# A two-layer decoder step on one core: 8 KB weight pieces, a longer weight ring, one sum for the samples' attention, and an earlier sort of the experts

## Chip, core and metric

One NeuronCore of a Trainium2 chip runs the whole step as one program. The metric is the device time of one execution in microseconds (us), the median of several runs. TensorE (PE) does the matrix products, VectorE (DVE) and ScalarE (ACT) the elementwise work, GpSimd (POOL) a part of that and the indirect DMAs, SyncE (SP) issues most of the other DMAs. Weights and tables come from HBM through 16 DMA engines that all queues share.

## What is computed

The step runs a prompt of 512 tokens and 8 samples of one token each through two layers with shared weights; the width is 1024. All data are fp32.

```python
# layer 0 mixer: convolution and differential attention; the samples read a paged cache of 1024 positions
gb, gc, xin, q, k, v = jnp.split(x @ w_in, EVEN_SPLITS, axis=-1)
a = jax.nn.softmax(s, axis=-1).reshape(b, H_B, 2, tq, tk)
a = a[:, :, 0] - lam * a[:, :, 1]
o = jnp.einsum('bhqk,bkhe->bqhe', a, v)            # H_B = 4 heads of 128 values
y = jnp.concatenate([y_conv, rms_norm(o, subln_w) ...], axis=-1) @ w_out
# layer 1 mixer: mLSTM in chunks
# tail of both layers
x = layer_norm(ALPHA * x + mix)
x = layer_norm(ALPHA * x + hier_moe(x))
x = x + sigmoid(x @ wpg) * (p @ wpp)

def hier_moe(x, ...):      # 4 groups of 4 experts: best group, two best experts in it
    for e in range(16):
        hid = silu(xt @ w_gate[e]) * (xt @ w_up[e])      # 1024 -> 512
        y = y + gate[:, e:e + 1] * (hid @ w_down[e])     # 512 -> 1024
```

## The kernel before

A layer is a mixer (layer 0's projections and attention to about 222 us, its output projection, "mix 0", to about 321 us), the experts (layer 0 to about 626 us; layer 1 from about 981 to 1288 us), and the tail with the gated projection of `p`.

**Experts.** They are done in 16 slots `e`. Slots 0 and 1 hold experts 0 and 1; slots 2 to 15 hold the others, sorted by the number of their tokens on the chip (`cnt`, `key`, `lt`, `sr`, `sel`, `eid`, lines 1143 to 1149), and the sorted numbers become integers in `eii` (line 1150). SP reads a number from `eii` into a register (line 1388) before it can issue that slot's loads. Odd slots from 3 on (`SMALL`) take up to 64 tokens and multiply in fp32 (lines 1253, 1297). The nine others, the dense slots, take up to 128 tokens and use three products of a high and a low part (`mm3`, lines 142 to 144); ACT and DVE make the two parts of each weight (lines 137 and 138). `prepare(e)` makes a slot's one-hot matrix `oh` (line 1088), its row indices `ix` (1099) and gathers its tokens from `xd` by an indirect DMA on POOL (1103). `tokens` transposes the gathered rows on PE (`tr_block`, line 266; the gathered rows are the stationary operand), `hidden` makes silu times up (its ACT step is line 1263 in dense slots), `hidden_T` transposes that, and `down` multiplies by the last weight and scatters the sum. Slot `e`'s down product stands behind slot `e+1`'s up product, except that slot 13's stands before slot 14's up product.

**Weight buffers.** A slot reads 6 MB: gate, up and down of 2 MB, each in two loads of 1 MB (`load_w`, line 155, issued by SP, some by POOL). A load goes to the next buffer of a ring (`wbuf`, `wpools`, `wturn`) and waits until whoever read the buffer's last content is done. The ring has 13 buffers of 1 MB: 3 of `wp2`, 4 of `wp3`, two halves of `wps[1]` ("b"), two of "xl" and two of "xh". Eight loads (gate and up of slots 0 and 1) are issued in the mixer. At slot `ESW = 10` the ring becomes `RS = "2b"`, which takes `wp2` (3 buffers) and the two halves of `wps[1]` in turn. In a load, partition `p` gets row `k*128+p` for each `k` ("(k p)"), so one contiguous piece is a row: 2 KB for gate and up, 4 KB for down.

**Samples' attention in mix 0.** The weights of all 8 samples stand in `a4`. `v_step` takes one sample `b`: eight products (line 669) of `a4` with the sample's cached values, in a PSUM tile of its own; a mask (line 673) that keeps this sample's rows and, per head, its columns; a product with a one-hot matrix (line 677) that sums over partitions; and an addition to `acco`. The values come by indirect DMAs on POOL, 2 MB a sample. `mix_tile` is a generator that makes the output projection for one of five row groups `m`; steps of the samples' attention run between its steps.

Of the kernel before, what the change touches and what calls it, by code (L numbers as in the profile page):

```python
# [14 lines left out]
OP = mybir.AluOpType  # L15
# [36 lines left out]
ESW = 10  # L52
G0 = 2
RS = "2b"
# [66 lines left out]
class K:  # L121
# [233 lines left out]
    def even(self):  # L355
# [5 lines left out]
        with tc.tile_pool(name="mz", bufs=1) as mz, tc.tile_pool(name="mx", bufs=1) as mx, tc.tile_pool(name="mx2", bufs=2) as mx2:  # L361
# [299 lines left out]
            def v_step():  # L661
                if not vq:
                    return
                b, wv = vq.pop(0)
                pv = self.tp()
                for hf in range(2):
                    w = wv[hf].rearrange("p (t c) -> p t c", t=4)
                    for t in range(4):
                        TE.matmul(pv[32 * t:32 * t + 32, :], self.a4[:, 4 * hf + t, :], w[:, t, :],
                                  start=(hf == 0), stop=(hf == 1))  # L670
                mk = mx2.tile([128, 512], F32, name="mk", bufs=1)
                h4 = lambda a: a.rearrange("p (h c) -> p h c", h=4)
                V.scalar_tensor_tensor(h4(mk), h4(pv), self.c("bmask")[:, b:b + 1],
                                       self.c("maskhp")[:, :, None].to_broadcast([128, 4, 128]), op0=OP.mult, op1=OP.mult)
                yield
                po = self.tp()
                TE.matmul(po[:NS, :], self.onf_b(mx, b), mk, start=True, stop=True)
                if b == 0:
                    V.tensor_copy(acco, po[:NS, :])
                else:  # L680
                    V.tensor_add(acco, acco, po[:NS, :])
# [40 lines left out]
            def decode_tail():  # L722

                while vq:
                    yield from v_step()
                    v_load()
                    yield
                os_ = mx2.tile([NS, 4, 128], F32, name="os", tag="aT")
                for h in range(4):
                    V.scalar_tensor_tensor(os_[:, h, :], vt[:NS, 4, h * 128:(h + 1) * 128], self.an[:, h:h + 1],  # L730
                                           acco[:, h * 128:(h + 1) * 128], op0=OP.mult, op1=OP.add)
                yield from norm_o(os_, NS, 4, 0, slice(TP, T))
                self.moe_load(0, 1 + NW2, 1 + NW2 + NW3)
# [24 lines left out]
    def onf_b(self, p, b):  # L758
        if b == 0:
            self.eb = p.tile([128, NS, NS], F32, name="eb")  # L760
            self.V.tensor_copy(self.eb, self.c("mask8").rearrange("p (a b) -> p a b", a=8))
        return self.eb[:, b, :]

# [16 lines left out]
    def moe_load(self, i, a, b):  # L780

        rows = lambda w: [w[h * 512:h * 512 + 512, :].rearrange("(k p) c -> p k c", p=128) for h in range(2)]
        ws = [v for e in range(2) for n in ("w_exp_gate", "w_exp_up") for v in rows(self.A[n][i, e])]
        self.early += [self.load_w(v) for v in ws[a:b]]
# [68 lines left out]
    def mix_all(self, i, y, tags, before, after_first, own=None):  # L853
# [3 lines left out]
        parts = self.mix_split(own)  # L857
        for _ in range(MS):
            next(parts)
# [15 lines left out]
    def mix_tile(self, i, m, y, tags, tile, before):  # L875
# [41 lines left out]
        acc = [self.acc() for _ in range(2)]  # L917
# [37 lines left out]
        if m == 0:  # L955
            for k in range(8):
                if k == 6:
                    while before():
                        self.advance()
                    load()  # L960
                for hf in range(2):
                    product(k, hf)
                yield
            add(0)
            add(1)
        else:
# [92 lines left out]
    def moe(self, i):  # L1059
# [5 lines left out]
        with tc.tile_pool(name="exp", bufs=2) as p2:  # L1065
# [58 lines left out]

            prepare(0)
            prepare(1)

            order = ExitStack()
            order.enter_context(tc.issue_after(self.ix_last.ins))
            order.enter_context(tc.issue_after(self.gather_last.ins))  # L1130
# [19 lines left out]
            V.tensor_copy(eii, eid[:, 2:])  # L1150
# [7 lines left out]

            rs = p2.tile([128, 5, ns], F32, name="rs", bufs=1)
# [54 lines left out]
            def tokens(xg, small=False):  # L1214

                if small:
                    xT = p2.tile([128, 4, 2, HCAP], F32, name="xT", tag="gh")
                    ps = self.tp().rearrange("p (a b) -> p a b", a=4)
                    for j in range(4):
                        self.tr_block(ps[:, j, :], xg[:, j * 128:(j + 1) * 128], 128)  # L1220
# [4 lines left out]
                for g in range(2):  # L1225
                    ps = self.tp().rearrange("p (a b) -> p a b", a=4)
                    for j in range(4):
                        self.tr_block(ps[:, j, :], xg[:, (g * 4 + j) * 128:(g * 4 + j + 1) * 128], 128)
# [38 lines left out]
            def hidden_T(hid, small=False):  # L1267
                if small:
                    hx = p2.tile([128, 4, HCAP], F32, name="hx", tag="hh", bufs=1)
                    ps = self.tp()[:, 0:4 * HCAP].rearrange("p (a b) -> p a b", a=4)  # L1270
                    for j in range(4):
                        self.tr_block(ps[:, j, :], hid[:, j * 128:(j + 1) * 128], HCAP)
# [5 lines left out]
                for j in range(4):  # L1278
                    self.tr_block(ps[:, j, :], hid[:, j * 128:(j + 1) * 128], 128)
# [3 lines left out]
            def down(ix, gate, hx, src, now, small, end=False):  # L1283

                pd = self.acc()
                ws = [self.load_w(v, now) for v in src] if end else None
# [30 lines left out]
            def dyn(ev, n, r):  # L1317

                return [A[n][i][bass.ds(ev, 1), h * r:h * r + r, :].rearrange("o (k p) c -> p (o k) c", p=128) for h in range(2)]
# [57 lines left out]
            rows = lambda w, n: [w[h * n:h * n + n, :].rearrange("(k p) c -> p k c", p=128) for h in range(2)]  # L1377
# [3 lines left out]
            for e in range(NE):  # L1381
# [8 lines left out]
                if e == ESW:  # L1390

                    self.wpools, self.wturn = self.ring(RS), 0
# [29 lines left out]
                if last and e != NE - 2:  # L1422
                    down(*last[:2], hx, *last[3])
# [627 lines left out]
```

## Time and profile before

| | before |
|---|---|
| median of 3 runs | 1384.08 us (1380.81 to 1386.75) |
| profiled execution | 1380.0 us, span 1378.2 us |
| PE busy | 1263.3 us, 92% of the span |
| DVE, ACT, POOL busy | 863.5, 628.7, 254.0 us |
| moved by DMA | 338.73 MB, mean 246 GB/s |

The span is the time from the first to the last event on the core. The busy share of an engine is a mean over the stages; what holds a stage is seen in its own windows and waits. The DMA share of a window is the mean busy share of the 16 DMA engines.

### The profile page before, as it was taken

Reading aid. Unit: us, or ns where it says so; the run is one execution under the profiler, and the core shown is the slowest. Engines: PE = TensorE matmul, PEld = TensorE weight load, DVE = VectorE, ACT = ScalarE, POOL = GpSimd, SP = SyncE. Lnnn points to the kernel's source line nnn. Section 1 sums busy time; section 2 is a strip of 40 time slices with the busy share of each in tenths; the row PEclk is TensorE's granted clock in tenths of the full one; section 3 lists DMA queues with packets and bytes.
Section 4 is the critical chain, followed back from the end, with each engine's and each line's share of the span. In section 5 each row is a group of like instructions: output and inputs, shape, how many; then the busy total and the mean of one; then the engine's idle time right before and its main releaser. Section 6 shows DMA issues by size and latency. Waiting matters only on the chain. (4 is left out here: it accounts for less than half of the span.)

```text
span 1378.2 us, 20912 instructions
## 1 busy us (share of the span) xinstructions
PE 1263.3 (92%) x7884; PEld 967.4 (70%) x7884; DVE 863.5 (63%) x1515; ACT 628.7 (46%) x1053; POOL 254.0 (18%) x242
## 2 busy tenths in 40 slices
PE   7989999995899999988999999999589999998897
PEld 7988876563766655547979999878367665555686
DVE  4689985557976654435645456874698565443572
ACT  3224664223665544436553333323366554443562
POOL 1033312314122221001230000112312112100113
PEclk9999999997999999999999999999789999999899
DMA  8568645873999989998332224493399999999911
GB/s 284 159 199 293 221 176 210 311 275 136 355 349 370 367 298 363 372 364 249 109 112 82 74 65 127 158 338 124 137 328 332 377 361 315 343 369 355 286 49 40
DMA packets 157449, 338.73 MB, mean 246 GB/s; under 512 B 16095, under 2 KB 54459, under 8 KB 153246
## 3 DMA queue, kind: packets, MB, share of 16 engines
q1 hardware_dynamic: 138974, 271.28, 55.3%
q0 software_dynamic: 18224, 65.98, 15.3%
q8 instruction: 64, 1.05, 0.3%
q14 instruction: 43, 0.35, 0.1%
q10 hardware_dynamic: 144, 0.07, 0.0%
HBM read 313.66 MB, written 32.81 MB: 251 GB/s over the span
## 5 line engine op out<-in xcount | busy, mean ns | idle before, releaser
L138 DVE TENSOR_TENSOR w<-w,sh 128x1024 fp32r<-128x1024 f32 x224 | 267.3, 1221 | 117.5 <-ACT sh L137 98.8
L137 ACT CAST sh<-w 128x1024 fp32r<-128x1024 f32 x224 | 227.9, 1048 | 175.8 <-PE acc L234 104.8
L143 PE MATMUL acc<-w,gh 128*128 128x512 f32 x288 | 119.2, 414 | 7.3 <-DVE w L138 7.3
L142 PE MATMUL acc<-sh,gh 128*128 128x512 f32 x288 | 118.6, 412 | 3.4 <-ACT sh L137 3.4
L144 PE MATMUL acc<-sh,gl 128*128 128x512 f32 x288 | 117.1, 407 | 0.0
L1253 PE MATMUL acc<-w,xT 128*64 128x512 f32 x432 | 109.7, 597 | 1.3 <-DMA w<-in_w_exp_up 1.3
L234 PE MATMUL acc<-xh,sh 128*128 128x256 f32 (+1 forms) x384 | 84.1, 296 | 5.8 <-ACT sh L137 2.6
L234 PE MATMUL acc<-x2h,w 128*128 128x256 f32 (+1 forms) x384 | 86.8, 288 | 1.6 <-DMA wgx<-in_w_ple_gate 0.8
L234 PE MATMUL acc<-xh,w 128*128 128x256 f32 (+1 forms) x384 | 80.3, 291 | 1.1 <-DVE w L138 1.1
L234 PE MATMUL acc<-x3h,sh 128*128 128x256 f32 (+1 forms) x384 | 81.1, 291 | 0.0
L234 PE MATMUL acc<-xl,sh 128*128 128x256 f32 (+1 forms) x384 | 80.6, 290 | 0.0
L234 PE MATMUL acc<-x3h,w 128*128 128x256 f32 (+1 forms) x384 | 78.5, 284 | 0.0
L234 PE MATMUL acc<-x3l,sh 128*128 128x256 f32 (+1 forms) x384 | 78.3, 284 | 0.0
L1253 PEld LDWEIGHTS acc<-w,xT 128*64 128x64 f32 x432 | 32.3, 136 | 59.6 <-issue 54.0
L1103 POOL DMA_INDIRECT w<-xd,ix x32 | 47.4, 1480 | 140.6 <-DVE gs L1113 84.1
L143 PEld LDWEIGHTS acc<-w,gh 128*128 128x128 f32 x288 | 56.3, 195 | 24.0 <-DVE w L138 11.3
L142 PEld LDWEIGHTS acc<-sh,gh 128*128 128x128 f32 x288 | 56.1, 195 | 18.6 <-ACT sh L137 5.2
L234 PEld LDWEIGHTS acc<-xh,sh 128*128 128x128 f32 x384 | 62.4, 195 | 7.6 <-ACT sh L137 2.9
L1314 POOL DMA_INDIRECT ya<-y,ix x18 | 29.3, 1627 | 205.7 <-ACT y L1313 205.7
L234 PEld LDWEIGHTS acc<-x2h,w 128*128 128x128 f32 x384 | 64.4, 188 | 2.5 <-issue 1.3
L144 PEld LDWEIGHTS acc<-sh,gl 128*128 128x128 f32 x288 | 56.4, 196 | 13.0
L234 PEld LDWEIGHTS acc<-xh,w 128*128 128x128 f32 x384 | 61.7, 194 | 1.4 <-DVE w L138 1.3
(540 smaller groups left out, 2932.5 us busy)
## 6 DMA issues: line engine op xcount, KB each, us to landing
w<-in_w_exp_gate SPq DMA_DIRECT2D x56, 1024.0 KB
w<-in_w_exp_up SPq DMA_DIRECT2D x50, 1024.0 KB
w<-in_w_exp_down SPq DMA_DIRECT2D x50, 1024.0 KB
wpair<-in_w_exp_up SPq DMA_DIRECT2D x14, 1024.0 KB
w<-in_w_in_even SPq DMA_DIRECT2D x12, 1024.0 KB
w<-in_w_in_odd SPq DMA_DIRECT2D x12, 1024.0 KB
wpair<-in_w_exp_down SPq DMA_DIRECT2D x10, 1024.0 KB
wpair<-in_w_exp_gate SPq DMA_DIRECT2D x8, 1024.0 KB
```

The source lines that it names most:

```text
L137: a = self.S.copy(h, src)
L138: self.sp_last = a, self.V.tensor_sub(l, src, h.bitcast(F32))
L142: self.T.matmul(ps, ah, bh, start=start, stop=False)
L143: self.T.matmul(ps, ah, bl, start=False, stop=False)
L144: self.mm3_last = self.T.matmul(ps, al, bh, start=False, stop=stop)
L234: self.mm_last = self.T.matmul(ps[t], a[:, k, :], b[:, k, t0[t]:t1[t]], start=(k == 0 and i == 0), stop=(k == nk - 1 and i == 2))
L1103: self.gather_last = G.indirect_dma_start(out=xg, out_offset=None, in_=rows2(xd) if small else xd, in_offset=bass.IndirectOffsetOnAxis(ap= ...
L1253: TE.matmul(ps[z * HCAP:(z + 1) * HCAP, :], xT[:, a, hf, :], ws[z][:, a, :], start=(hf == 0 and a == 0), stop=(hf == 1 and a == 3))
L1314: G.indirect_dma_start(out=ya, out_offset=bass.IndirectOffsetOnAxis(ap=ix[:, 0:1], axis=0), in_=y, in_offset=None, bounds_check=T - 1, oob ...
```

## The change

Five edits. (1) The ring of 13 buffers stays until slot 13, and then goes on in the same order without "b" and "xh" (9 buffers), where before it was exchanged for "2b" at slot 10. (2) In a load, partition `p` gets neighbouring rows ("(p k)"), so that its piece is 8 KB for gate, up and down; to match, the transposes take every fourth column of the gathered rows (16 bytes apart) and every second column of the hidden values (8 bytes apart). (3) The samples' weights are masked per sample (`ab`, 128x256 elements on DVE) before the products; all samples add into one PSUM tile, half of the accumulator `macc[0]`, and one `v_sum` masks heads and sums over partitions. `macc` is one pair of accumulators for all row groups, and group 0's residual addition comes before its last `yield`. (4) The sort by counts stands between `prepare(0)` and `prepare(1)`. (5) The four down loads of slots 0 and 1 (`wd`) are issued before `prepare(0)`, slot 0's on POOL and slot 1's on SP.

```diff
@@
-ESW = 10
+ESW = 13
 G0 = 2
-RS = "2b"
...
@@ v_step, v_sum
                 b, wv = vq.pop(0)
-                pv = self.tp()
+
+                if b == 0:
+                    self.ab = mx2.tile([128, 2, 8, NS, 4], F32, name="ab", tag="mk", bufs=1)
+                ab = self.ab[:, b % 2]
+                V.tensor_tensor(ab, self.a4.rearrange("p t (b h) -> p t b h", h=4),
+                                self.c("mask8").rearrange("p (a b) -> p a b", a=8)[:, b, None, :, None].to_broadcast([128, 8, NS, 4]), op=OP.mult)
+                ab = ab.rearrange("p t b h -> p t (b h)")
+                yield
+                pv = self.macc[0][:, 1, :]
                 for hf in range(2):
                     w = wv[hf].rearrange("p (t c) -> p t c", t=4)
                     for t in range(4):
-                        TE.matmul(pv[32 * t:32 * t + 32, :], self.a4[:, 4 * hf + t, :], w[:, t, :],
-                                  start=(hf == 0), stop=(hf == 1))
+                        TE.matmul(pv[32 * t:32 * t + 32, :], ab[:, 4 * hf + t, :], w[:, t, :],
+                                  start=(b == 0 and hf == 0), stop=(b == NS - 1 and hf == 1))
+
+            def v_sum():
                 mk = mx2.tile([128, 512], F32, name="mk", bufs=1)
                 h4 = lambda a: a.rearrange("p (h c) -> p h c", h=4)
-                V.scalar_tensor_tensor(h4(mk), h4(pv), self.c("bmask")[:, b:b + 1],
-                                       self.c("maskhp")[:, :, None].to_broadcast([128, 4, 128]), op0=OP.mult, op1=OP.mult)
+                V.tensor_tensor(h4(mk), h4(self.macc[0][:, 1, :]), self.c("maskhp")[:, :, None].to_broadcast([128, 4, 128]), op=OP.mult)
                 yield
                 po = self.tp()
-                TE.matmul(po[:NS, :], self.onf_b(mx, b), mk, start=True, stop=True)
-                if b == 0:
-                    V.tensor_copy(acco, po[:NS, :])
-                else:
-                    V.tensor_add(acco, acco, po[:NS, :])
+                TE.matmul(po[:NS, :], self.c("bmask"), mk, start=True, stop=True)
+                V.tensor_copy(acco, po[:NS, :])
@@ decode_tail
+                yield from v_sum()
...
@@ moe_load, moe (rows, dyn)
-        rows = lambda w: [w[h * 512:h * 512 + 512, :].rearrange("(k p) c -> p k c", p=128) for h in range(2)]
+        rows = lambda w: [w[h * 512:h * 512 + 512, :].rearrange("(p k) c -> p k c", p=128) for h in range(2)]
...
-                return [A[n][i][bass.ds(ev, 1), h * r:h * r + r, :].rearrange("o (k p) c -> p (o k) c", p=128) for h in range(2)]
+                return [A[n][i][bass.ds(ev, 1), h * r:h * r + r, :].rearrange("o (p k) c -> p (o k) c", p=128) for h in range(2)]
@@ moe
+            rows = lambda w, n: [w[h * n:h * n + n, :].rearrange("(p k) c -> p k c", p=128) for h in range(2)]
+            wd = [[self.load_w(v, z == 1) for v in rows(A["w_exp_down"][i, z], 256)] for z in range(2)]
             prepare(0)
-            prepare(1)
-
-            order = ExitStack()
-            order.enter_context(tc.issue_after(self.ix_last.ins))
-            order.enter_context(tc.issue_after(self.gather_last.ins))
+            first = ExitStack()
+            first.enter_context(tc.issue_after(self.ix_last.ins))
...
-            V.tensor_copy(eii, eid[:, 2:])
+            eii_last = V.tensor_copy(eii, eid[:, 2:])
...
+            first.enter_context(tc.issue_after(eii_last.ins))
+            prepare(1)
+            first.close()
+
+            order = ExitStack()
+            order.enter_context(tc.issue_after(self.ix_last.ins))
+            order.enter_context(tc.issue_after(self.gather_last.ins))
@@ tokens, hidden_T (the small and the dense form alike)
-                        self.tr_block(ps[:, j, :], xg[:, (g * 4 + j) * 128:(g * 4 + j + 1) * 128], 128)
+                        self.tr_block(ps[:, j, :], xg[:, g * 512 + j:(g + 1) * 512:4], 128)
...
-                    self.tr_block(ps[:, j, :], hid[:, j * 128:(j + 1) * 128], 128)
+                    self.tr_block(ps[:, j, :], hid[:, j // 2 * 256 + j % 2:(j // 2 + 1) * 256:2], 128)
@@ loop over slots
                 if e == ESW:
 
-                    self.wpools, self.wturn = self.ring(RS), 0
+                    k, ws = self.wturn % len(self.wpools), self.wpools
+                    self.wpools, self.wturn = [w for w in ws[k:] + ws[:k] if w not in (self.wps[1], "xh")], 0
...
-                    down(*last[:2], hx, *last[3])
+                    down(*last[:2], hx, *last[3], ws=wd[e - 1] if e < 3 else None)
```

PE's program in mix 0 has, before, products by `a` (the tile `a4`; `w` are the cached values) into a `tps` tile, and behind them the sum over partitions (L677); L142 to L144 are the output projection.

```order
L142 MATMUL acc<-xl,yh 128x512
L143 MATMUL acc<-w,yh 128x512
L144 MATMUL acc<-xl,yl 128x512
L677 MATMUL tps<-mk,eb 8x512
L266 MATMUL tps<-cst,xw_2651 128x128 x4
L142 MATMUL acc<-xh,yh 128x512
L143 MATMUL acc<-w,yh 128x512
L144 MATMUL acc<-xh,yl 128x512
L142 MATMUL acc<-xh,yh 128x512
L143 MATMUL acc<-w,yh 128x512
L144 MATMUL acc<-xh,yl 128x512
L669 MATMUL tps<-w,a_2548 32x512 x8
```

The program of the change has at that place products by the masked `ab` straight into the accumulator, and no sum behind them.

```order
L265 MATMUL tps<-cst,xw_2651 128x128 x4
L141 MATMUL acc<-xh,yh 128x512
L142 MATMUL acc<-w,yh 128x512
L143 MATMUL acc<-xh,yl 128x512
L141 MATMUL acc<-xh,yh 128x512
L142 MATMUL acc<-w,yh 128x512
L143 MATMUL acc<-xh,yl 128x512
L676 MATMUL acc<-w,ab 32x512 x8
```

The eight L677 products are gone from between the projection's products; one sum (L685) comes after the last sample, and the eight products by the values are as many as before, of the same shape.

SP's program where layer 0's experts begin, before: the last rows of the mixer's result (`xd`, `ya`), then the first expert number and slot 2's loads.

```order
L1006 DMA xd_90<-xw_3231 8x1024
L1008 DMA ya_92<-xw_3231 8x1024
L1388 TENSOR_LOAD eii
L1388 ISA x2
L155 ISA
L155 DMA wpair<-in_w_exp_gate 128x4x512
L155 ISA
L155 DMA wpair<-in_w_exp_gate 128x4x512
L155 ISA
L155 DMA wpair<-in_w_exp_up 128x4x512
```

The same place in the change, as far as the second of the register loads that now follow one another:

```order
L154 DMA wpair<-in_w_exp_down 128x2048 x2
L1009 DMA xd_90<-xw_3189 8x1024
L1011 DMA ya_92<-xw_3189 8x1024
L1397 TENSOR_LOAD eii
L1397 ISA x2
L154 ISA
L154 DMA wpair<-in_w_exp_gate 128x2048
L154 ISA
L154 DMA wpair<-in_w_exp_gate 128x2048
L1397 TENSOR_LOAD eii
L1397 ISA x2
L1397 TENSOR_LOAD eii
```

Slot 1's two down loads moved ahead of the stores of the last rows, and the other 13 reads of `eii`, which stood one before each later slot's loads, moved up: nine stand between slot 2's last gate load and its first up load, and four behind the next read of a number (`nbi`).

DVE's program at that place, before: behind the rank of the tokens (`rank`) come both slots' `oh` and `ix`, and the sort is mixed with other routing work, so that `eii` is written 23 rows behind `rank`.

```order
L1056 SCALAR_TENSOR_TENSOR rank<-tps,Mb 128x80
L1088 TENSOR_TENSOR oh<-slf,rank 128x640 x2
L1099 TENSOR_SCALAR ix<-tps 128x1 x2
L1165 TENSOR_REDUCE sgx<-L 128x5
L1143 COPY cnt<-tps 128x16
L1166 TENSOR_TENSOR sge<-L,sgx 128x20
L1165 TENSOR_REDUCE sex<-el 128x5
L1144 SCALAR_TENSOR_TENSOR key<-cnt,cst 128x16
```

In the change:

```order
L1059 SCALAR_TENSOR_TENSOR rank<-tps,Mb 128x80
L1091 TENSOR_TENSOR oh<-slf,rank 128x640
L1102 TENSOR_SCALAR ix<-tps 128x1
L1146 COPY cnt<-tps 128x16
L1147 SCALAR_TENSOR_TENSOR key<-cnt,cst 128x16
L1148 TENSOR_TENSOR lt<-key 128x196
L1149 TENSOR_REDUCE sr<-lt 128x14
L1150 TENSOR_TENSOR sel<-sr,cst 128x196
L1151 TENSOR_TENSOR lt<-sel,cst 128x196
L1152 TENSOR_REDUCE eid<-lt 128x14
L1153 CAST eii<-eid 128x14
L1091 TENSOR_TENSOR oh<-slf,rank 128x640
```

The sort now follows slot 0's indices at once, and slot 1's `oh` and `ix` come behind `eii`.

## Rows read from the trace of the kernel before

**Rows 1.** windows of 25 us in layer 0's experts (engines busy, clock, DMA share, GB/s).

```profile
450.00:475.00 25.00, 25.00 (x127) 13.97 (x127) 13.76 (x19) 10.83 (x15) 5.39 (x3) 1.00 1.03 367
...
575.00:600.00 25.00, 21.24 (x91) 14.50 (x92) 15.01 (x14) 14.26 (x17) 3.12 (x2) 0.93 1.05 377
```

**Rows 2.** timeline of ACT, layer 0: the hidden activations of slots 4 to 14.

```profile
423.73 0.60 ACT L1263 ACTIVATE hid<-acc 128x512 f32<-128x512 f32 x1 [1.77 <-PE acc L144]
...
455.76 0.60 ACT L1263 ACTIVATE hid<-acc 128x512 f32<-128x512 f32 x1 [4.97 <-PE acc L144]
...
487.74 0.60 ACT L1263 ACTIVATE hid<-acc 128x512 f32<-128x512 f32 x1 [4.91 <-PE acc L144]
...
522.50 0.60 ACT L1263 ACTIVATE hid<-acc 128x512 f32<-128x512 f32 x1 [4.58 <-PE acc L144]
...
559.76 0.60 ACT L1263 ACTIVATE hid<-acc 128x512 f32<-128x512 f32 x1 [4.49 <-PE acc L144]
...
602.66 0.60 ACT L1263 ACTIVATE hid<-acc 128x512 f32<-128x512 f32 x1 [4.72 <-PE acc L144]
```

**Rows 3.** the same in layer 1: slots 8 and 14.

```profile
1149.10 0.60 ACT L1263 ACTIVATE hid<-acc 128x512 f32<-128x512 f32 x1 [4.91 <-PE acc L144]
...
1264.72 0.60 ACT L1263 ACTIVATE hid<-acc 128x512 f32<-128x512 f32 x1 [5.34 <-PE acc L144]
```

**Rows 4.** waits of SP's queue, 345 to 615 us: line <- releaser: total us, times, longest.

```profile
SPq L155 <- DVE w L138: 84.6, 23, 8.1
SPq L155 <- PE acc L1253: 51.6, 13, 10.7
```

**Rows 5.** timeline of SP around slot 10: weight loads as they are issued.

```profile
478.99 6.16 SPq L155 DMA_DIRECT2D w<-in_w_exp_down  x2
...
498.14 0.99 SPq L155 DMA_DIRECT2D w<-in_w_exp_gate  x2
```

**Rows 6.** windows of 5 us (columns as in the first group).

```profile
275.00:280.00 5.00, 4.90 (x25) 2.15 (x23) 2.82 (x5) 0.59 (x1) 0.99 (x1) 1.00 1.01 408
...
490.00:495.00 5.00, 4.86 (x41) 2.44 (x41) 1.10 (x2) 2.09 (x4) 0.64 (x1) 1.00 0.65 255
...
505.00:510.00 5.00, 4.78 (x21) 3.56 (x21) 4.97 (x8) 3.75 (x4) 1.43 (x1) 1.00 1.05 395
```

**Rows 7.** timeline of PE: slot 13's down product.

```profile
589.09 3.65 PE L1297 MATMUL acc<-w,hx 128*64 128x512 f32 x16
```

**Rows 8.** mix 0: PE's groups and a timeline of PE.

```profile
L677 PE MATMUL tps<-mk,eb 128*8 128x512 f32 x16 | 8.2, 594 | 0.0
...
248.98 1.02 PE L677 MATMUL tps<-mk,eb 128*8 128x512 f32 x2
249.94 0.66 PE L266 MATMUL tps<-cst,xw 128*128 128x128 f32 x4
```

**Rows 9.** the 25-us window in mix 0's middle.

```profile
250.00:275.00 25.00, 25.00 (x144) 12.78 (x144) 12.61 (x19) 5.30 (x7) 9.96 (x9) 1.00 0.88 321
```

**Rows 10.** transposes on PE's timeline; loads of stationary operands in the experts and mix 0.

```profile
432.22 1.09 PE L266 MATMUL tps<-cst,w 128*128 128x128 f32 x8
433.15 0.39 PE L1093 MATMUL tps<-idr,oh 128*128 128x1 bf16 x10
...
L266 PEld LDWEIGHTS tps<-cst,w 128*128 128x128 f32 x84 | 9.6, 141 | 5.8 <-issue 4.9
...
L934 PEld LDWEIGHTS acc<-w,yh 128*8 128x8 f32 x14 | 1.3, 90 | 1.3
```

**Rows 11.** timelines of DVE, SP and PE at layer 0's first slots.

```profile
338.27 0.17 DVE L1150 CAST eii<-eid 128x14 int32<-128x14 f32 x1
...
327.15 0.29 SPq L1006 DMA_DIRECT2D xd<-xw  x1
...
336.93 2.79 PE L266 MATMUL tps<-cst,w 128*128 128x128 f32 x12 [4.64 <-DMA w<-xd,ix]
```

**Rows 12.** SP's register loads of an expert number, all 28.

```profile
L1388 SPq TENSOR_LOAD <-eii x28: 262/274/1084, 338.6 to 1249.8; - x28
```

More of the change, by code (lines that the diff above doesn't have):

```diff
@@ L756, in even @@
             self.mix_all(0, y, tags, lambda: self.pend, after_first)
[L758 to L762, printed above, removed]
     def mixer_pools(self):
@@ L857, in mix_all @@
         parts = self.mix_split(own)
+        self.macc = [self.acc() for _ in range(2)]
         for _ in range(MS):
@@ L916, in mix_tile @@
             y_split(1)
-        acc = [self.acc() for _ in range(2)]
+        acc = self.macc
         st = tile("lst", [128, 2, 6], F32)
@@ L962, in mix_tile @@
                     product(k, hf)
-                yield
+                if k < 7:
+                    yield
             add(0)
             add(1)
+            yield
         else:
@@ L1219, in tokens @@
                     for j in range(4):
-                        self.tr_block(ps[:, j, :], xg[:, j * 128:(j + 1) * 128], 128)
+                        self.tr_block(ps[:, j, :], xg[:, j::4], 128)
                     S.copy(xT.rearrange("p a z b -> p a (z b)"), ps)
@@ L1271, in hidden_T @@
                     for j in range(4):
-                        self.tr_block(ps[:, j, :], hid[:, j * 128:(j + 1) * 128], HCAP)
+                        self.tr_block(ps[:, j, :], hid[:, j // 2 * 256 + j % 2:(j // 2 + 1) * 256:2], HCAP)
                     self.hid_last = S.copy(hx, ps)
@@ L1278, in hidden_T, with down @@
                 for j in range(4):
-                    self.tr_block(ps[:, j, :], hid[:, j * 128:(j + 1) * 128], 128)
+                    self.tr_block(ps[:, j, :], hid[:, j // 2 * 256 + j % 2:(j // 2 + 1) * 256:2], 128)
                 self.hid_last = self.split(hh, hl, ps)
                 return hh, hl
-            def down(ix, gate, hx, src, now, small, end=False):
+            def down(ix, gate, hx, src, now, small, end=False, ws=None):
                 pd = self.acc()
-                ws = [self.load_w(v, now) for v in src] if end else None
+                ws = [self.load_w(v, now) for v in src] if end else ws
                 if end:
@@ L1375, in overflow @@
                         down(ix, gate, hidden_T(hidden(pgu)), dyn(ev, "w_exp_down", 256), True, False)
-            rows = lambda w, n: [w[h * n:h * n + n, :].rearrange("(k p) c -> p k c", p=128) for h in range(2)]
             last = None
```

## The prediction

> **What bounds the kernel now.** Busy shares first: PE is busy for 92% of the span, so time is won only by taking work from PE, or where PE waits or runs slower than it could. Next I looked for stretches of the second kind, in windows over the experts of layer 0. At 450 to 475 us PE is busy for 25.00 of 25 us at full granted clock (1.00). At 575 to 600 us it is busy for 21.24 at a mean clock of 0.93, while the DMA engines stand at 1.05 [rows 1]. So the experts are bound by PE at first and by their weights at the end.
>
> The size of that is read from the hidden activation of every second slot, since a dense and a small slot make a pair with equal work. From slot 4 to 6 it takes 32.03 us, from 6 to 8 31.98, then 34.76, 37.26 and 42.90 [rows 2]. 32.0 us is what a pair takes where PE never waits. Layer 1 behaves alike: from slot 8 to 14 it takes 115.62 us [rows 3], in layer 0 114.92.
>
> Why do the weights come late? SP's queue, which issues the loads, waits mostly for readers of old buffers: 84.6 us for DVE's splitting and 51.6 us for the small slots' products [rows 4]. At slot 10 the change of the ring is seen: after the down loads issued at 478.99 us nothing is issued until 498.14 us [rows 5], because the short ring first has to wait for buffers that are still to be read. In that hole the DMA share falls to 0.65 (255 GB/s), and then it is at 1.05 [rows 6], too late to make up for it. So at the end DMA bandwidth is the limit, but the loss began as a want of free buffers.
>
> **1 and 2. The ring and the pieces.** With 13 buffers until slot 13 the hole at 484 to 498 us is not there. Can the DMA then keep up? A pair needs 12 loads, 12.58 MB. With 2 KB pieces the engines moved 395 GB/s at a share of 1.05, that is 376 at 1.00 [rows 6], so 33.5 us a pair. To that come its gathers and scatters: 192 rows of 4 KB in and as many out, 1.6 MB, 4.2 us at that rate. 37.7 us against PE's 32.0: the store of loaded weights shrinks by 5.7 us a pair. The windows agree that it shrinks: 367 GB/s [rows 1] are 11.7 MB in 32 us, less than the weights alone. With the early down loads 12 MB are in the buffers at the start, 32 us of PE's work; over the 6 pairs from slot 2 to 14 that would be used up (34 us). Now the pieces: the gathers of cached values in mix 0 bring 8 KB pieces already, 408 GB/s at 1.01, 404 at 1.00 [rows 6]. A pair's weights then take 31.1 us, with the 4.2 us 35.3, and 6 pairs use 20 of the 32 us. So with both edits the weights stay ahead of PE to the end; the pieces have no term of their own, but without them the last pair would lose some us. From slot 13 on nine buffers are left, 24 us of PE's work, and the switch itself forces no wait, since the order goes on.
>
> Slot 14's pair is longer than 32.0 also when PE is the limit, since slot 13's down product stands ahead of its up product: 3.65 us [rows 7]. Three pairs then take 3 x 32.0 + 3.65 = 99.65 us, where before they took 114.92 and 115.62. That is **-15.3** in layer 0 and **-16.0** in layer 1. Bounds: nothing is won (new holes), or all of it.
>
> The price of the pieces is on PE. The transposes of gathered rows now read every fourth column as the stationary operand. There are 9 x 8 + 7 x 4 = 100 of them in a layer, 200 in all, and 64 in a layer of hidden values at every second column. Eight take 433.15 - 432.22 = 0.93 us, 0.116 us each, and loading such an operand takes 141 ns beside the products [rows 10]. No operand of PE in this kernel is read with a stride, so the price is bounded. Below: nothing, since the same columns go into the same array. Above: a load of 8 columns takes 90 ns, one of 128 takes 141 [rows 10], so the columns themselves cost (141 - 90) / 120 = 0.42 ns each, 54 ns for 128; if reading takes four times as long, as wide as the stride, that is 163 ns more for each, 33 us for 200. PE has no slack there [rows 1], so it would all be paid. I take **0**: nearer to the lower end, since most of the 141 ns does not depend on the columns, and the product of the transpose before runs meanwhile.
>
> [...]
>
> **3. Samples' attention.** PE loses 7 of the 8 sums over partitions. A sum takes two passes, from 248.98 to 249.94 us, 0.96 us in all, and the 16 rows are all there are [rows 8]: 7 x 0.96 = 6.7 us of PE's time. The eight products a sample stay. PE is full in the middle of mix 0 (25.00 of 25 us), so this comes off the end unless something else is just behind. The DMA is at 0.88 there with 321 GB/s [rows 9]: it can run 12% faster and no more, and each sample's 2 MB must come before the next step. In 99 us PE can win 6.7%, so the gathers come near their limit without reaching it. I take three quarters, **-5.0**; bounds 0 (the gathers are the limit) and -6.7. On DVE the eight masks of `ab` have 256 columns where the removed ones had 512, so DVE gets no more work (12.61 of 25 us busy [rows 9]).
>
> **4 and 5. Sort and early down loads.** At the start of layer 0's experts `eii` is written at 338.27 us while PE begins its transposes at 336.93 after a wait of 4.64 us for slot 0's gathered rows [rows 11]. PE thus does not wait for the sort. With the sort earlier, some 4 us of it, slot 2's loads come 4 us earlier, which feeds the store and not PE. Against it stand three delays. Slot 1's indices and gather come behind the sort, 2 to 4 us later, and its transposes stand early in PE's order, so PE can wait for them: 0 to 2 us. Nine register loads of an expert number (each 0.27 us, with what belongs to it about 0.45 [rows 12]) now stand between two loads, 4 us of SP, covered by slot 2's 2 MB of gate weights and slot 1's 2 MB in flight. The last stores to `xd` (327.15 us [rows 11]) are issued behind slot 1's two down loads on the same queue, and the gathers wait for these stores: 2 MB at 404 GB/s is 5 us if the queue serves strictly in order, nothing if the down loads have gone out before. I take **+1.0** for both layers together, with bounds -4 and +8.
>
> **The sum.** 1380.0 us is the profiled execution's own time. 1380.0 - 15.3 - 16.0 - 5.0 + 1.0 = 1344.7 us. The runs' median is 1384.1, 4.1 us above the profiled one, so I forecast **1349 us**, 2.5% less. A difference under 0.5% (7 us) is about what a measurement here cannot tell from none.
>
> **The rivals.**
>
> *A. The strided transposes are slow.* For it speaks that the load of the operand (141 ns) is longer than the spacing (116 ns), so little can be hidden behind the product; against it that only 54 ns of it are columns. Twice the reading is 200 x 0.054 = 11 us, 1356, on the median's basis **1360 us**; three times 22 us, **1371 us**; four times 33 us, **1382 us**.
>
> *B. The same, so slow that the kernel loses.* The gain of the other parts is 35.3 us, so this decides from 35.3 / 200 = 0.18 us more for each transpose, a spacing of 0.29 us. If the whole spacing of 0.116 us grows with the stride, four times, it is 0.35 x 200 = 70 us: 1415, on the median's basis **1419 us**. The other engines could hide nothing of it, as PE is the limit; for it speaks only that nothing here shows such a read.
>
> *C. The DMA stays the limit at the end.* If the pairs from slot 8 on go on taking 34.76 us, as the pair before the hole's effect shows in full [rows 2], three of them and slot 13's product take 107.9 us: 7.0 us are won in layer 0 and 7.7 in layer 1. With mix 0's 5 and the start's 1 it would be 1380.0 - 18.7 = 1361, on the median's basis **1365 us**. For it speaks a share that is at 1.03 already while PE is full [rows 1], and that the store is counted from estimates: at the old rate it is used up just at slot 14. Against it stand the 12 us that the pieces leave.
>
> *D. The ring does what it should, and mix 0 and the starts give it back.* The gathers limit mix 0 (nothing won) and the stores behind the down loads cost 4 us in each layer: 1380.0 - 31.3 + 8 = 1357, on the median's basis **1361 us**.
>
> **Chances and range.** The forecast's case (1336 to 1357) has 0.60, A 0.16, C 0.11, D 0.07, B 0.06. The lower end takes the whole of mix 0 (-1.7 more), the start's -4 (5 less than taken) and 6 us for stretches whose clock no longer drops: 1336. The upper end takes in A at three times the reading with 6 us on top: 1377. Outside are B and the upper part of A. Faster by over 0.5% are the forecast, C, D and A up to three times: 0.87. A at four times is within 0.5%: 0.07. B is slower: 0.06.
>
> **What would show it.** The ring: pairs of 32.0 us up to slot 12, about 35.7 to slot 14, no hole in SP's loads near slot 10, PE busy for all of 25 us at 575 us, DMA share under 1. The pieces: rates near 404 GB/s at a share of 1.00 in the experts. The strides: eight transposes at a spacing of 0.12 us (right), of 0.17 to 0.28 (A) or more (B); then pairs get longer everywhere, by 12 transposes' extra. Mix 0: shorter by 5 us, one L685 in place of eight sums, its DMA share near 0.95; a share at 1.0 with PE waiting for cached values is D. The starts: `eii` at about 334 us, first product no later than 339 us. The forecast is wrong if the transposes are slow, or if the nine buffers at the end leave a new hole.

## The result, and the profile after

The change is slower: 1397.94 us (median of 4 runs, 1397.11 to 1402.96) against 1382.44 us of before in the same rounds, a ratio of 1.011 (1.008 to 1.015). The forecast was 1349 us, 2.5% faster.

The profiled execution has a span of 1401.2 us, 23.0 more than before. In order of time: 3.4 us arise ahead of mix 0, where nothing was changed (PE's granted clock is 0.50 from 108.7 to 115.5 us, where before has 1.00). Mix 0 takes as long as before (-0.3). The first hidden activation of layer 0 comes 2.5 us later behind mix 0; from it to slot 15's, the experts take 258.2 us in place of 251.5. Near 710 us, in layer 1's mixer, 3.3 us are won back; layer 1 then starts its experts 6.9 us later and needs 258.8 us in place of 252.0 for them.

The timeline of ACT in the changed kernel, layer 0. The rows with `hid` on 128x512 answer to [rows 2]; the others show what stands around the hidden activation of two small slots, 5 (443.49) and 9 (511.90).

```profile
439.99 1.99 ACT L136 CAST sh<-w 128x1024 fp32r<-128x1024 f32 x2
443.49 0.59 ACT L1270 ACTIVATE hid<-acc 64x512 f32<-64x512 f32 x1 [1.50 <-PE acc L1263]
445.03 1.05 ACT L136 CAST sh<-w 128x1024 fp32r<-128x1024 f32 x1 [0.96 <-PE acc L143]
...
462.14 0.60 ACT L1273 ACTIVATE hid<-acc 128x512 f32<-128x512 f32 x1 [5.00 <-PE acc L143]
...
496.92 0.60 ACT L1273 ACTIVATE hid<-acc 128x512 f32<-128x512 f32 x1 [4.60 <-PE acc L143]
...
511.90 0.59 ACT L1270 ACTIVATE hid<-acc 64x512 f32<-64x512 f32 x1 [6.78 <-PE acc L1263]
512.39 1.98 ACT L136 CAST sh<-w 128x1024 fp32r<-128x1024 f32 x2
...
534.05 0.60 ACT L1273 ACTIVATE hid<-acc 128x512 f32<-128x512 f32 x1 [4.58 <-PE acc L143]
...
571.33 0.60 ACT L1273 ACTIVATE hid<-acc 128x512 f32<-128x512 f32 x1 [4.60 <-PE acc L143]
...
614.53 0.60 ACT L1273 ACTIVATE hid<-acc 128x512 f32<-128x512 f32 x1 [5.45 <-PE acc L143]
```

Pairs from slot 6 on take 34.78, 37.13, 37.28 and 43.20 us; before it was 31.98, 34.76, 37.26, 42.90 [rows 2]. The slow pairs thus begin one pair earlier, and the fast one before them (32.5, to 462.14) is half a microsecond longer. In slot 5 the splits of the waiting down weights are done when the hidden activation starts; in slot 9 ACT has been idle for 6.78 us and begins the splits only behind it; they stand behind it in the program, and no wait for a transfer is recorded ahead of them. PE's timeline shows what goes with this.

```profile
438.23 1.23 PE L265 MATMUL tps<-cst,w 128*128 128x128 f32 x8
439.30 0.39 PE L1096 MATMUL tps<-idr,oh 128*128 128x1 bf16 x10
...
442.81 0.60 PE L1263 MATMUL acc<-w,xT 128*64 128x512 f32 x2
443.34 0.50 PE L141 MATMUL acc<-sh,hh 128*128 128x512 f32 x1
...
445.39 0.69 PE L265 MATMUL tps<-cst,hid 64*128 64x64 f32 x4
...
507.41 4.45 PE L1263 MATMUL acc<-w,xT 128*64 128x512 f32 x18
513.27 0.69 PE L265 MATMUL tps<-cst,hid 64*128 64x64 f32 x4 [1.41 <-DVE hid L1271]
...
515.09 0.77 PE L142 MATMUL acc<-w,hh 128*128 128x512 f32 x1
515.66 0.63 PE L143 MATMUL acc<-sh,hl 128*128 128x512 f32 x1
```

At 443 us the waiting down product (L141) follows the up product (L1263) at once, and the transposes of slot 5's own hidden values (`hid`) come eight products later, when ACT and DVE have made them. At 512 us there are no split weights yet, and on PE the transposes of `hid` come next: PE stops for 1.41 us until DVE has made slot 9's hidden values, and then a product takes 0.63 us where it otherwise takes 0.40. So the late order is one of PE's program as well as of ACT's. Windows of the same kernel (columns as in [rows 1]):

```profile
375.00:400.00 25.00, 25.00 (x128) 20.61 (x127) 23.67 (x25) 19.95 (x22) 3.55 (x2) 1.00 0.54 174
475.00:500.00 25.00, 23.17 (x115) 16.17 (x113) 16.21 (x17) 14.65 (x17) 3.23 (x3) 1.00 1.02 404
...
514.00:518.00 4.00, 4.00 (x27) 3.40 (x28) 3.97 (x7) 3.25 (x5) 1.45 (x1) 0.61 1.02 430
```

From 514 to 518 us the granted clock is 0.61 of full: from 514.9 to 518.3 us, behind the stop, it is 0.50, and 1.00 again from there to 519. Not every such stop has this: the pair with slot 7, with a stop of 1.45 us, has a mean granted clock of 1.00 and takes 34.78 us, the pair with slot 9 has 0.95 and takes 37.13. In the slow stretch the DMA engines are at 1.02 with 404 GB/s, and from 375 to 400 us at 0.54 with 174. The issues on SP's queue tell why:

```profile
381.82 0.33 SPq L154 DMA_DIRECT2D w<-in_w_exp_gate  x1
399.14 0.33 SPq L154 DMA_DIRECT2D wpair<-in_w_exp_gate  x1
...
563.90 2.60 SPq L154 DMA_DIRECT2D w<-in_w_exp_gate  x2
581.78 0.87 SPq L154 DMA_DIRECT2D wpair<-in_w_exp_down  x2
...
996.94 0.81 SPq L154 DMA_DIRECT2D wpair<-in_w_exp_down  x2
997.88 0.30 SPq L1009 DMA_DIRECT2D xd<-xw  x1
```

Nothing is issued for 17 us from 382 us on: slot 1's early down weights lie in the next buffers of the ring, and are split only shortly before. A second hole of 15 us (566.5 to 581.78) stands where the ring is cut to nine buffers. The last pair of rows shows the stores to `xd` behind the early down loads in layer 1; the gather there is issued at 1006.17 us, 8.3 us behind the store, where it was 4.7 (987.64 to 992.34).

But do the engines wait for weights in the slow stretch? The waits from 490 to 570 us (engine, line, releaser: total us, times, longest):

```profile
ACT hid L1270 <- PE acc L1263: 13.6, 2, 6.8
...
PE tps L265 <- DVE hid L1271: 2.8, 2, 1.4
...
PEld acc L1263 <- DMA wpair<-in_w_exp_down: 0.3, 1, 0.3
```

The last line is the only wait of PE, ACT or DVE for a transfer in these 80 us. So a DMA share of 1.01, their mean, did not mean that the engines waited for it.

### The profile page after: what moved, and what is told of

It is laid out like the page before. It is cut to its first block, busy times and chain, and to the rows that moved or that the text cites. A ratio compares the mean times of both kernels' runs of the same rounds, so it can differ in the third digit from the quotient of the medians.

```text
span 1401.2 us, 20881 instructions
## 1 busy us (share of the span) xinstructions
PE 1272.4 (91%) x7870; PEld 981.9 (70%) x7870; DVE 855.5 (61%) x1508; ACT 627.2 (45%) x1053; POOL 254.2 (18%) x242
## 3 DMA queue, kind: packets, MB, share of 16 engines
q8 instruction: 64, 1.05, 0.3%
## 5 line engine op out<-in xcount | busy, mean ns | idle before, releaser
L137 DVE TENSOR_TENSOR w<-w,sh 128x1024 fp32r<-128x1024 f32 x220 | 261.9, 1222 | 114.0 <-ACT sh L136 100.0
L136 ACT CAST sh<-w 128x1024 fp32r<-128x1024 f32 x220 | 223.4, 1048 | 177.3 <-PE acc L233 104.1
L142 PE MATMUL acc<-w,gh 128*128 128x512 f32 x288 | 118.9, 413 | 8.9 <-DVE w L137 8.9
L141 PE MATMUL acc<-sh,gh 128*128 128x512 f32 x288 | 117.5, 408 | 3.4 <-ACT sh L136 3.4
L1263 PE MATMUL acc<-w,xT 128*64 128x512 f32 x384 | 101.0, 596 | 0.0
L142 PEld LDWEIGHTS acc<-w,gh 128*128 128x128 f32 x288 | 55.8, 194 | 26.5 <-DVE w L137 14.0
L265 PEld LDWEIGHTS tps<-cst,w 128*128 128x128 f32 (+1 forms) x296 | 41.8, 188 | 38.4 <-issue 29.0
L141 PEld LDWEIGHTS acc<-sh,gh 128*128 128x128 f32 x288 | 55.5, 193 | 18.8 <-ACT sh L136 5.2
L265 PE MATMUL tps<-cst,w 128*128 128x128 f32 (+1 forms) x296 | 53.1, 303 | 17.0 <-DMA w<-xd,ix 14.9
L1263 PEld LDWEIGHTS acc<-w,xT 128*64 128x64 f32 x384 | 30.2, 137 | 52.3 <-issue 50.9
```

The source lines that it names most:

```text
L136: a = self.S.copy(h, src)
L137: self.sp_last = a, self.V.tensor_sub(l, src, h.bitcast(F32))
L141: self.T.matmul(ps, ah, bh, start=start, stop=False)
L142: self.T.matmul(ps, ah, bl, start=False, stop=False)
L265: self.T.transpose(out, in_, self.c("ident")[:k, :k])
L1263: TE.matmul(ps[z * HCAP:(z + 1) * HCAP, :], xT[:, a, hf, :], ws[z][:, a, :], start=(hf == 0 and a == 0), stop=(hf == 1 and a == 3))
```

## Experiments

Theories: **1**, the early down loads sit in ring buffers that are read late, and hold up the queue. **2**, the strided transposes eat the gain on PE. **3**, the volume of the DMA is the limit whatever the order. **4** came with the first four runs: the order of splits and hidden activation on ACT ("early order": the splits ahead of it). Ratios are to the kernel before in the same rounds.

**a_late_down**, without the early down loads.

```diff
-            wd = [[self.load_w(v, z == 1) for v in rows(A["w_exp_down"][i, z], 256)] for z in range(2)]
...
-                    down(*last[:2], hx, *last[3], ws=wd[e - 1] if e < 3 else None)
+                    down(*last[:2], hx, *last[3])
```

> The change without the early down loads of slots 0 and 1 (each is loaded behind the next slot's up weights, as before). Theory 1, order in the ring: slot 1's early down loads sit in two ring buffers that are read only at 396 us, and the next load for these buffers holds up all loads behind it (nothing issued from 382 to 399 us, DMA share 0.54), and on SP's queue they delay the last stores of the mixer. Then the hole goes, the first product of both layers comes 3 to 6 us earlier, and the weights are ahead of PE longer: 15 to 30 us less than the change, 0.98 to 0.99 of before. Theory 2, the strided transposes cost PE the gain: nothing but the starts, 5 to 9 us less than the change, 1.005 of before. Theory 3, the DMA volume is the limit whatever the order: 1.00 to 1.005.

1380.37 us, 1.000 (0.997 to 1.003). The early loads cost 1.15%, some 16 us, but the rest of the change gains nothing. The experts of layer 0 take 250.4 us from first to last hidden activation, in place of 258.2.

**a_old_ring**, the change with `ESW = 10` and the ring "2b".

> The change with the short ring from slot 10 on, as before. Theory 1: the hole at 382 to 399 us stays and a second one comes at slot 10: 5 to 12 us more than the change, 1.015 to 1.02 of before. Theory 2: the ring hardly matters, since PE is the limit: the same as the change, 1.01. Theory 3: the same or up to 5 us more.

1403.82 us, 1.015 (1.012 to 1.019): in the change the longer ring is worth some 0.4%, no more than the noise of the two measurements, and not 2.2%.

**a_old_pieces**, the change with "(k p)" and plain transposes.

> The change with pieces of 2 and 4 KB and plain transposes. Theory 1: the late part of the experts is bound by the DMA, and at 376 in place of 400 GB/s a pair takes some 39.5 us in place of 37.1: 10 to 20 us more than the change, 1.02 to 1.025 of before. Theory 2: the strides are gone, and so is the loss: 10 us less than the change or better, 1.00 to 1.005. Theory 3: as theory 1.

1399.56 us, 1.013 (1.009 to 1.016), not told apart from the change itself. Theory 2 falls; so does the 1.02 of theories 1 and 3.

**b_ring**, the kernel before with the ring edit alone.

```diff
-ESW = 10
+ESW = 13
...
-                    self.wpools, self.wturn = self.ring(RS), 0
+                    k, ws = self.wturn % len(self.wpools), self.wpools
+                    self.wpools, self.wturn = [w for w in ws[k:] + ws[:k] if w not in (self.wps[1], "xh")], 0
```

> The kernel before with only the longer ring (13 buffers until slot 13, then nine in order). Theory 1: the hole at 484 to 498 us goes, and pairs behind slot 8 take 35 to 37 us at the old rate of the DMA in place of 34.8, 37.3 and 42.9: 10 to 20 us less than before, 0.985 to 0.993. Theory 2: the ring is worth what was forecast, up to 30 us, 0.978. Theory 3: 0.998 to 1.00.

1377.03 us, 0.996 (0.994 to 0.998). The hole in the loads is gone, but ACT's timeline has the pairs at 34.75 and 35.10 us:

```profile
487.13 0.60 ACT L1263 ACTIVATE hid<-acc 128x512 f32<-128x512 f32 x1 [4.91 <-PE acc L144]
...
521.88 0.60 ACT L1263 ACTIVATE hid<-acc 128x512 f32<-128x512 f32 x1 [4.58 <-PE acc L144]
...
556.98 0.60 ACT L1263 ACTIVATE hid<-acc 128x512 f32<-128x512 f32 x1 [4.60 <-PE acc L144]
```

From 490 to 570 us no engine waits for a transfer here, and still a pair takes 3 us more than 32.0. So I compared the programs. ACT's order between the hidden activations of slots 6 and 7, before:

```
L1263 ACTIVATE hid<-acc 128x512
L137 CAST hh<-tps 128x512
L1309 ACTIVATE y<-acc,gs 128x512
L137 CAST sh<-w 128x1024 x2
L137 CAST gh<-tps 128x512 x2
L137 CAST sh<-w 128x1024 x2
L1260 ACTIVATE hid<-acc 64x512
```

and in the change:

```
L1273 ACTIVATE hid<-acc 128x512
L136 CAST hh<-tps 128x512
L1319 ACTIVATE y<-acc,gs 128x512
L136 CAST gh<-tps 128x512 x2
L1270 ACTIVATE hid<-acc 64x512
L136 CAST sh<-w 128x1024 x2
L1231 COPY xT<-tps 128x512
L136 CAST sh<-w 128x1024 x4
```

The four splits (`sh`) of slot 6's down weights stood ahead of slot 7's hidden activation; now they stand behind it. Before has this late order from slot 9 on, the change from slot 7 on. The build, which places each engine's instructions, chooses it, and it is theory 4.

**b_presplit**, the kernel before with the early order in all small slots. `down_split` loads and splits what `down` did, earlier in the program. SP's program stays the same row by row, here and in the other runs with this edit; DVE, PE and POOL get another order together with ACT.

```diff
+                pre = down_split(*last[3]) if small else None
+                with ExitStack() as st:
+                    if pre:
+                        st.enter_context(tc.issue_after(self.sp_last[0].ins))
+                    hid = hidden(pgu, small)
                 if last and e != NE - 2:
-                    down(*last[:2], hx, *last[3])
+                    down(*last[:2], hx, *last[3], pre=pre)
```

> The kernel before with one thing changed: in small slots the four splits of the waiting down weights stand ahead of the hidden activation on ACT, as the build had them by itself up to slot 7, and not behind it, as it has them from slot 9 on. Theory 4, the order on ACT: pairs from slot 8 on take longer because PE ends the small slot's up product with no split weights at hand, stops, and goes on at half its clock. Then the pairs of slots 8 to 14 take 2 to 4 us less each, 1366 to 1376 us, 0.988 to 0.996 of before; the rest is lost to weights that come late behind the hole at slot 10. Theory 3, the DMA volume is the limit: the order is only a picture of late weights, 0.998 to 1.002.

1383.36 us, 0.999 (0.996 to 1.002). The pair from slot 8 to 10 falls from 34.76 to 33.28 us, but the later ones do not. Its waits from 530 to 570 us:

```profile
DVE w L138 <- ACT sh L137: 10.6, 3, 8.4
ACT sh L137 <- DMA w<-in_w_exp_down: 10.1, 2, 9.0
```

Now that ACT asks for the weights in time, they are late. Behind the order's limit stood that of the loads.

**b_ring_presplit**, both on the kernel before.

> The longer ring and that order together, on the kernel before. Theory 4: with the hole at slot 10 gone as well, pairs come near 32 us up to slot 12: 8 to 12 us a layer, 1358 to 1368 us, 0.982 to 0.989 of before, more than the two alone add up to. Theory 3: as the ring alone, 0.996.

1373.13 us, 0.993 (0.991 to 0.995): 32.66 us for the pair to slot 10, then 36.20, and from 490 to 570 us waits for down weights of up to 6.5 us remain. This is less than theory 4 alone forecast: with pieces of 2 and 4 KB the weights do not come in time.

**a_late_down_old_sort**, the change without early loads and earlier sort (`prepare(1)` back behind `prepare(0)`).

> The change without the early down loads and without the earlier sort. If the earlier sort itself delays the first slots (slot 1's indices and gather behind it, its transposes early on PE), both layers' experts start 4 to 5 us earlier than in the run without the early down loads: 1369 to 1374 us, 0.991 to 0.994 of before. If that delay belongs to something else (the samples' sum, the pieces), 0.999 to 1.00 again.

1375.25 us, 0.996 (0.994 to 0.998), 0.4% better than with the earlier sort: it did delay the first slots. From the last store to `xd` to the first hidden activation the profiles have 34.0 and 34.3 us in the two layers, in place of 38.7 and 36.9 (a_late_down).

**b_samples**, the kernel before with the samples' attention of the change.

> The kernel before with only the samples' attention changed. If the seven removed sums are worth PE's time, as forecast, mix 0 ends 5 us earlier, 0.9965 of before. If the start of mix 0 loses what they give (the first sample's products now stand behind all of group 0's products, so PE idles and its clock falls while it waits for group 0's rows), 0.998 to 1.00.

1379.39 us, 0.998 (0.995 to 1.000): at most 6 us, not told from nothing. Mix 0 is not shorter in its profile.

**c_presplit**, the change without early loads and earlier sort, and with the early order on ACT.

> The change without the early down loads and the earlier sort, and with the splits of the down weights ahead of the small slots' hidden activation. Theory 4 (order on ACT) with the weights' rate: with 2 KB pieces the engines then waited up to 9 us for down weights behind slot 10; at 400 GB/s they should not, and pairs take some 32.5 to 33.5 us up to slot 12: 1360 to 1366 us, 0.983 to 0.988 of before. If the weights' rate does not matter, as without that order, 0.992 to 0.993.

1355.41 us, 0.978 (0.974 to 0.982), with the next run the fastest version, and 5 us below what was expected. ACT's timeline:

```profile
494.06 0.60 ACT L1268 ACTIVATE hid<-acc 128x512 f32<-128x512 f32 x1 [4.95 <-PE acc L143]
...
526.96 0.60 ACT L1268 ACTIVATE hid<-acc 128x512 f32<-128x512 f32 x1 [4.58 <-PE acc L143]
...
560.83 0.60 ACT L1268 ACTIVATE hid<-acc 128x512 f32<-128x512 f32 x1 [4.60 <-PE acc L143]
...
599.91 0.60 ACT L1268 ACTIVATE hid<-acc 128x512 f32<-128x512 f32 x1 [4.15 <-PE acc L143]
```

32.90 and 33.87 us a pair, near the 32.0 that was forecast, but 39.08 for the last, where about 35.7 was forecast. From 490 to 570 us its engines wait 1.4 us for one transfer.

**c_presplit_esw15**, the same with the ring cut at slot 15.

> The same, with the ring of 13 buffers cut to nine at slot 15 and not at slot 13, where SP issued nothing for 17 us. If that hole delays slots 14 and 15, 3 to 6 us a layer less than the run with the cut at slot 13, 0.977 to 0.983 of before; if the loads behind the cut are early enough, the same as it.

1355.82 us, 0.979 (0.975 to 0.983): the same. The hole at the cut costs nothing that can be measured.

**a_presplit**, the change itself with the early order.

> The change itself with that order on ACT. If the early down loads cost their 16 us through the order that the build then chose (the splits behind the hidden activation from slot 7 on, two slots earlier than before), most of it comes back: 1380 to 1386 us, 0.998 to 1.003 of before. If they cost it through the hole in the loads at slot 4, the engines now wait for weights in place of each other: 1394 to 1400 us, 1.008 to 1.013.

1380.02 us, 0.995 (0.993 to 0.998), 22 us less than the change. SP's program is the same row by row; ACT, DVE and PE have another order. ACT's timeline:

```profile
504.90 2.00 ACT L136 CAST sh<-w 128x1024 fp32r<-128x1024 f32 x2 [0.96 <-DMA w<-in_w_exp_down]
507.40 1.99 ACT L136 CAST sh<-w 128x1024 fp32r<-128x1024 f32 x2 [0.51 <-DMA w<-in_w_exp_down]
510.72 0.59 ACT L1270 ACTIVATE hid<-acc 64x512 f32<-64x512 f32 x1 [1.33 <-PE acc L1263]
```

Four splits ahead of slot 9's hidden activation, small waits for weights (the hole at slot 4 is still there), and pairs of 34.04 and 33.75 us in place of 37.13 and 37.28.

The time is at the edge of the first range, but it does not show that the early loads cost through the order: the edit also mends the slots from 9 on, which are late in before too. What shows it is c_presplit, with the same order and without the early loads and the earlier sort. Layer 0 in a_presplit, the last store to `xd` and the first and last hidden activation:

```profile
329.36 0.30 SPq L1009 DMA_DIRECT2D xd<-xw  x1
...
366.73 0.60 ACT L1273 ACTIVATE hid<-acc 128x512 f32<-128x512 f32 x1
...
614.88 0.59 ACT L1270 ACTIVATE hid<-acc 64x512 f32<-64x512 f32 x1
```

and in c_presplit:

```profile
331.89 0.29 SPq L1009 DMA_DIRECT2D xd<-xw  x1
...
365.06 0.60 ACT L1268 ACTIVATE hid<-acc 128x512 f32<-128x512 f32 x1
...
609.18 0.59 ACT L1265 ACTIVATE hid<-acc 64x512 f32<-64x512 f32 x1 [2.75 <-PE acc L1258]
```

To the first activation 37.4 us in place of 33.2, through the slots 248.2 in place of 244.1; in layer 1 40.1 in place of 34.2, and 251.7 in place of 244.7. That is 21 us, as much as the two spans differ by, with the early order on both sides.

**b_pieces**, the kernel before with 8 KB pieces and strided transposes.

> The kernel before with 8 KB pieces and strided transposes alone. The order on ACT is that of before. The strides cost 0.46 us a pair (32.5 in place of 32.0), some 7 us in all; what the engines waited for weights behind slot 10 (2 us a layer) goes: 1.001 to 1.004 of before. If faster loads help the late slots, as forecast, 0.985 to 0.995.

1383.07 us, 0.999 (0.997 to 1.002). The pair from slot 6 to 8, in which PE never waits, takes 32.50 us in place of 31.98:

```profile
465.42 0.60 ACT L1263 ACTIVATE hid<-acc 128x512 f32<-128x512 f32 x1 [5.01 <-PE acc L144]
...
497.92 0.60 ACT L1263 ACTIVATE hid<-acc 128x512 f32<-128x512 f32 x1 [4.94 <-PE acc L144]
```

That is the strides' price, some 7 us in all by this pair. The whole kernel is not slower beyond its interval of 3.5 us, so something gives most of that back. The late pairs of layer 0 show little of it (36.13, 37.15 and 42.47 us in place of 34.76, 37.26 and 42.90); where it comes from was not traced.

## Why the prediction was wrong

**The step that failed** is the reading of what bounds the late slots: "So at the end DMA bandwidth is the limit, but the loss began as a want of free buffers." It rested on a DMA share of 1.05 beside a PE that was not full [rows 1] and on the hole in SP's loads [rows 5]. The ring edit, priced by it at -31.3 us, measured -5 (b_ring), though the hole was gone. The runs put the build's order in its place: in small slots from 9 on, before has the splits of the waiting down weights behind the hidden activation on ACT, and on PE the transposes of the hidden values directly behind the up product, so that PE stops there for 1.4 us. Mending this is worth 22 us in the change (a_presplit), and some 24 us where the early loads and the earlier sort are left out (a_late_down_old_sort against c_presplit). ACT's and PE's order changed together, so which of the two counts is not shown.

The weights were a second limit just behind it: in before the order alone gains nothing (b_presplit), and behind the longer ring 0.3% (b_ring_presplit). With the change's pieces and samples' attention as well, ring and order give 30 us less than before (c_presplit). Even then the slots do not win what was forecast: the three late pairs take 105.9 us in layer 0 and 107.6 in layer 1, 9 and 8 us less than before, in place of 15.3 and 16.0. The pair of 34.76 us, which rival C took for the DMA's work, is for the most part the order's: 32.66 us in b_ring_presplit. A slower kernel had a chance of 0.06, and only by rival B, with transposes 0.29 us apart; they stand 0.134 us apart (rival A, below), so no rival held what made it slower.

**Early down loads**, priced within +1.0 for parts 4 and 5 (bounds -4 and +8), cost 16 us. The prediction counted them as twelve buffers full at the start and did not ask in which turn they are read: the ring hands out buffers in the order of the loads. With the early loads the build has the late order from slot 7 on (also in a_old_ring and a_old_pieces), without them from slot 9 at the earliest; why was not examined. But the order is not what they cost: with it mended on both sides, early loads and earlier sort still cost 1.75% (0.995 against 0.978), 24 us, no less than the 1.6% between the change and a_late_down_old_sort. Half of that arises between the last store to `xd` and the first hidden activation, half within the slots. What the hole, the stores and the sort each take of it was not separated.

**The earlier sort** cost 0.4%, about 6 us, in place of "0 to 2 us" for slot 1's transposes and a gain of the store; the 4 us by which slot 2's loads come earlier were worth nothing, as forecast. **The stores behind the down loads** were seen in layer 1 (8.3 us to the gather in place of 4.7), close to the 4 us of rival D.

**The strides** (rival A) are real and small: eight transposes take 1.07 us in place of 0.93, and loading the operand takes longer in both kinds. Groups of the changed kernel, 340 to 640 us:

```profile
L265 PEld LDWEIGHTS tps<-cst,w 128*128 128x128 f32 x100 | 15.2, 210 | 14.6 <-issue 10.1 <-DMA w<-xd,ix 4.1
...
L265 PEld LDWEIGHTS tps<-cst,hid 64*128 64x128 f32 x28 | 3.9, 208 | 12.2 <-DVE hid L1271 11.9 <-issue 0.4
```

210 ns and 208 ns in place of 141 [rows 10] and 138 is the reading, which A estimated at 54 ns, twice over and a little more, but the spacing grew by only 0.018 us: some 0.05 of the 0.069 us do not show in it. Loads run beside products (from 375 to 400 us PEld is busy for 20.61 and PE for 25.00 of 25 us). A pair pays 0.5 us, 7 to 8 us in all, against A's 11.

**The rate of 8 KB pieces** was nearly right (404 GB/s at 1.02, so 396 at 1.00), and so was that it gives no time of its own (b_pieces). With the order mended, pieces and samples' attention together give 1.5% (b_ring_presplit against c_presplit), and the samples' attention alone gave 0.2%. **Mix 0**, priced at -5.0, gave -0.3 in the profile and at most 6 us alone. Its products by the values now begin at 246.76 us, behind all of group 0's; the gain was lost inside mix 0, but by what was not tested.

The signed terms, from differences of ratios: early loads +16, sort +6, ring -5, samples -3, pieces and strides -1, together +13; measured +16 with 4.5 us of uncertainty.

## What to carry to other kernels

Here a DMA share of 1.01 over 80 us stood beside one wait for a transfer, of 0.3 us: look for a wait that ends with a transfer before pricing a load. Where a build places the instructions of every engine, compare the order of every engine in a fast and a slow repetition of the same work, also on engines that the change does not touch; here such an order, of four rows on ACT and of what moved with them on PE and DVE, was worth 22 us. A run that mends two things at once does not say which of them was broken: it takes a second run with the same mend and without the suspect. In a ring, load in the order in which buffers are read free: here two loads moved ahead held up all behind them on SP's queue for 17 us.

## What the runs showed of the hardware

Loading a stationary operand of 128 columns took 141 ns for the gathered rows and 138 ns for the hidden values of small slots in the kernel before, 210 ns and 208 ns in the change, where the columns stand 16 and 8 bytes apart: 69 and 70 ns more, so the two strides cost the same here. After a stop of 1.41 us in slot 9 of the change, PE's granted clock stood at 0.61 from 514 to 518 us; after a stop of the same length in slot 9 of the kernel before it stayed at 1.00:

```profile
502.96 0.46 PE L266 MATMUL tps<-cst,hid 64*128 64x64 f32 x4 [1.41 <-DVE hid L1261]
...
503.00:507.00 4.00, 4.00 (x35) 3.41 (x36) 3.83 (x6) 3.68 (x6) 0.98 (x1) 1.00 1.03 377
```

Against 32.49 us, a pair of the change with such a stop was 2.3 us longer where the clock stayed (34.78 us, mean clock 1.00), and 4.6 us longer where it fell (37.13 us, 0.95).
